# The last layer's first lower projections by Strassen's algorithm, with the plain pairs' rows written as right factors

## The chip, the cores and the metric

The kernel runs on one core of a Trainium2 chip. The metric is the device time of one execution in microseconds (us); lower is better. The core's engines have queues of their own, each worked off in order, and meet by semaphores: TensorE (PE) multiplies, VectorE (DVE) and ScalarE (ACT) do elementwise work, GpSimd (POOL) does elementwise work and issues the DMAs that accumulate, SyncE (SP) issues the other loads.

## What is computed

A trunk of two layers over 512 tokens of 1024 features, all in float32: a Conformer convolution layer, then a layer with sliding-window attention, each followed by a SwiGLU feed-forward part with 2816 hidden features. The change lies in the feed-forward part of the last layer:

```python
D_FF = -(-8 * D_MODEL // (3 * 256)) * 256        # 2816
...
def swiglu_ffn(x, w_up, w_down):
    gate, up = jnp.split(x @ w_up, 2, axis=-1)
    return (jax.nn.silu(gate) * up) @ w_down
...
        h = h + swiglu_ffn(rmsnorm(h, norm_ffn[l]), ffn_w_up[l], ffn_w_down[l])
    return rmsnorm(h, norm_final)
```

## The kernel before

Every matmul of float32 data is done as three matmuls on split values: a value is a high part (rounded for the PE) and a remainder, and the product is high x high, high x remainder and remainder x high (`mm3`, lines 383 to 385). Weights are split on the chip: `split_chunk` casts a chunk of 128 x 1024 to its high part `whi` on ACT and subtracts it on DVE to give `wlo` (line 307). There are five buffers of each, four (`raw`) for what is loaded, and a cast into a buffer waits until the PE has read the chunk that lay there before.

The 2816 hidden features are 11 pairs of 256. A pair's upper projection is done in one of two ways. *Plain* (`ffn_up`): four chunks, 24 matmuls of 512 columns each; `evac` scales the four banks on DVE (lines 637 and 639), applies SiLU on ACT (638), multiplies on POOL (640) and splits the result into `hid`. *By Strassen's algorithm* (`ffn_prod`): the 512 tokens are cut into two halves, and seven products of 24 matmuls of 256 columns take the place of eight; a product needs a combination of weight blocks and a combination of activations. I call them upper products 0 to 6. The blocks of a weight matrix lie in a tile `blocks` (three blocks, two buffers) and two `raw` tiles; SP loads them, and POOL issues DMAs that add one block onto another (`load_block`, line 241); two sums are left to DVE (lines 256 and 257). The activations' combinations, the right factors, are built once per layer by `right_factors`, called step by step through a background list while the plain pairs run; the two tiles it works in come from the pools `blocks` and `hid`.

The lower projection, too, is plain (`down_group`: chunks of 24 matmuls of 512 columns) or by Strassen's algorithm (`down_prod`: for each of two row groups, seven products of 18 matmuls of 256 columns over three pairs; I call those of the first group lower products, in the order 0, 1, 3, 2, 4, 5, 6). Its right factors are combinations of the hidden rows by token halves, kept by the class `Rights`: `finish` makes four subtractions of 256 columns on DVE and splits the seven factors of a pair.

Before, the last layer's part 0 (pairs 0 to 2) has two plain pairs, whose factors for the upper products are built meanwhile, then pair 2 by Strassen's algorithm, then a plain lower projection over the three pairs. Parts 1 and 2 (pairs 3 to 8) use Strassen's algorithm both ways, and pairs 9 and 10 end in a plain lower projection that is joined with the final normalization.

The order in each queue is not the order of the source: the scheduling layer moves instructions by its own estimate of their times, and the order is then fixed in the program.

Of the kernel before, what the change touches and what calls it, by code (L numbers as in the profile page):

```python
# [35 lines left out]
PLAIN = (2, 2)  # L36
# [21 lines left out]
def chunk_plan():  # L58
    plan = []

    def pw1():
        plan.extend(("pw1", ct, half) for ct in range(KT) for half in range(2))

    def pw2():
        for g in range(2):
            for kp in range(KT // 2):
                plan.append(("pw2", kp, g))

    def ups(layer, lo, hi):
        for pair in range(lo, hi):  # L70
            if pair >= PLAIN[layer]:
                plan.extend(("prod", layer, pair, j) for j in range(7))
                continue
            for half in range(2):
                for which in range(2):
                    plan.append(("up", layer, pair, half, which))

    def ffn(layer, lo, hi):
        ups(layer, lo, hi)
        if lo:  # L80
            plan.extend(("dprod", layer, (lo, ms), j) for ms in range(2) for j in D_ORDER)
            return
        for g in range(2):
            for kp in range(lo, hi):
                plan.append(("down", layer, kp, g))

    pw1()
    pw2()
    for part in HALVES0:
        ffn(0, *part)  # L90
    for part in range(2):
        for half in range(2):
            plan.append(("kv", part, half))
    for quarter in range(4):
        for half in range(2):
            plan.append(("q", half, quarter))
    for part in range(2):
        for g in range(2):
            for kp in range(2):
                plan.append(("o", part * 2 + kp, g))  # L100
    for part in HALVES1:
        ffn(1, *part)
    ups(1, *LAST)
    for kp in range(*LAST):
        for g in range(2):
            plan.append(("down", 1, kp, g))
    return plan
# [77 lines left out]
def hybrid_trunk(ctx: ExitStack, tc: tile.TileContext, xT, W, prm_in, wdw_in, rnd_in, sinks, relb, onehot, fin, out):  # L185
    nc = tc.nc
# [161 lines left out]
    def flush():  # L348
        for j in jobs:
            for _ in j[0]:  # L350
                pass
        jobs.clear()
        tick(1 << 30)
# [146 lines left out]
    def split(dst, src):  # L500
        nc.scalar.copy(dst[0], src)  # L501
        nc.vector.tensor_sub(dst[1], src, f32(dst[0]))  # L502
# [25 lines left out]
    def ffn_part(layer, part, xg, rms=None, on_h=None, right=None):  # L528
        lo, hi = (HALVES0, HALVES1)[layer][part]
        if lo:  # L530
            down_prod(layer, lo, ffn_prod(layer, lo, hi, xg, Rights()), on_h)
            return
        plain = PLAIN[layer]
        hids = [ffn_up(layer, lo, plain, xg, rms)]
        if hi > plain:
            flush()
            hids.append(ffn_prod(layer, plain, hi, right))
        hid = [t for pairs, n in zip(hids, (plain - lo, hi - plain)) for t in (pairs[i] for i in range(2 * n))]
        for g in range(2):
            banks = down_group([(("down", layer, kp, g), 2 * (kp - lo)) for kp in range(lo, hi)], lambda kt: hid[kt])  # L540
            for m in range(4):
                t = h[g * 4 + m]
                nc.vector.tensor_add(t, banks[m], t)
                if on_h is not None:
                    on_h(g * 4 + m)

    def halves(t):
        return t.rearrange("p (m s) -> p m s", m=2)
# [78 lines left out]
                for m in range(2):  # L627
                    on_h(4 + 2 * ms + m)

    def ffn_up(layer, lo, hi, xg, rms):  # L630
        hid = Act(2 * (hi - lo))

        def evac(pair, banks):
            rs_bc = rms.step2()
            for m in range(2):
                t1, t2 = temp(), temp()
                nc.vector.tensor_mul(t1, banks[m], rs_bc)
                nc.scalar.activation(t1, t1, AF.Silu)
                nc.vector.tensor_mul(t2, banks[2 + m], rs_bc)
                nc.gpsimd.tensor_mul(t2, t1, t2)  # L640
                split(hid[2 * (pair - lo) + m], t2)

        for pair in range(lo, hi):
            banks = [bank() for _ in range(4)]
            for half in range(2):
                for which in range(2):
                    whi, wlo = get("up", layer, pair, half, which)
                    order = [(k, m) for k in range(4) for m in range(2)]
                    if half == 1:
                        order = [(k, m) for m in range(2) for k in range(4)]  # L650
                    for k, m in order:
                        sl = slice(m * P, (m + 1) * P)
                        mm3(banks[which * 2 + m], (whi[:, k, sl], wlo[:, k, sl]), xg[half * 4 + k],
                            half == 0 and k == 0, half == 1 and k == 3)
                    if half == 0 and which == 1:
                        rms.step1()
            evac(pair, banks)
        return hid
# [122 lines left out]
    with conv_stage:  # L781
# [309 lines left out]
        b = None  # L1091
# [381 lines left out]
```

## Time and profile before

| | before |
|---|---|
| time, median of 3 runs | 1048.17 us (1048.11 to 1048.46) |
| the profiled execution: its time, its span | 1048.24 us, 1046.5 us |
| PE: chain that ended last, share | 86% |
| last layer's feed-forward part on PE, from the first plain pair to the last upper product | 695 to 1006 us |
| HBM traffic | 148 GB/s over the span |

The profile is one execution. Busy shares are per engine; a matmul's own duration is longer than the distance to the next one, since matmuls overlap. A release in square brackets names what ended an engine's idle time and how long that was.

### The profile page before, as it was taken

Reading aid. Unit: us, or ns where it says so; the run is one execution under the profiler, and the core shown is the slowest. Engines: PE = TensorE matmul, PEld = TensorE weight load, DVE = VectorE, ACT = ScalarE, POOL = GpSimd, SP = SyncE. Lnnn points to the kernel's source line nnn. Section 1 sums busy time; section 2 is a strip of 40 time slices with the busy share of each in tenths; the row PEclk is TensorE's granted clock in tenths of the full one; section 3 lists DMA queues with packets and bytes.
Section 4 is the critical chain, followed back from the end, with each engine's and each line's share of the span. In section 5 each row is a group of like instructions: output and inputs, shape, how many; then the busy total and the mean of one; then the engine's idle time right before and its main releaser. Section 6 shows DMA issues by size and latency. Waiting matters only on the chain.

```text
span 1046.5 us, 17698 instructions
## 1 busy us (share of the span) xinstructions
PE 1028.9 (98%) x7034; PEld 917.4 (88%) x7034; DVE 811.2 (78%) x1125; ACT 540.7 (52%) x835; POOL 237.8 (23%) x256
## 2 busy tenths in 40 slices
PE   9999999999999999999979999999999999999997
PEld 7756568888999999999969777788989999999996
DVE  8889867588789888978993767577965888788863
ACT  6565745353554455455562766354633554554443
POOL 0799801321010100101060433141100001010000
PEclk9999999999999999999999999999999999999999
DMA  7756533465557965976362211441654549667612
GB/s 254 201 146 164 133 114 92 129 161 141 167 159 173 281 165 124 260 194 161 82 217 72 72 41 42 147 135 41 188 174 122 141 121 263 174 153 176 178 46 81
DMA packets 51054, 153.95 MB, mean 147 GB/s; under 512 B 5979, under 2 KB 8844, under 8 KB 50956
## 3 DMA queue, kind: packets, MB, share of 16 engines
q1 hardware_dynamic: 41756, 124.79, 37.1%
q0 software_dynamic: 8064, 26.74, 15.1%
q10 hardware_dynamic: 1152, 1.29, 0.4%
q8 instruction: 55, 0.90, 0.3%
q14 instruction: 27, 0.22, 0.1%
HBM read 148.46 MB, written 6.83 MB: 148 GB/s over the span
## 4 chain that ended last, share of the span: by engine, by line
PE 86%; DVE 3%; issue 1%; POOL 1%; ACT 1%; POOLq 0%; ACTq 0%
PE bank L384 23%; PE bank L385 23%; PE bank L383 22%; PE bank L375 16%; PE bank L1402 2%; DVE quad L498 1%; DVE wlo L307 1%; DVE bank L318 1%; POOL quad L959 0%; DVE quad L991 0%; PE bank L472 0%; PE bank L489 0%; PE bank L1392 0%; DVE h L596 0%; POOL quad L978 0%
## 5 line engine op out<-in xcount | busy, mean ns | idle before, releaser
L384 PE MATMUL bank<-quad,whi 128*128 128x256 f32 (+1 forms) x1572 | 473.7, 303 | 4.1 <-DVE quad L498 4.1
L385 PE MATMUL bank<-quad,wlo 128*128 128x256 f32 (+1 forms) x1572 | 470.4, 303 | 0.0
L383 PE MATMUL bank<-quad,whi 128*128 128x256 f32 (+1 forms) x1572 | 465.9, 302 | 1.9 <-ACT quad L497 1.9
L384 PEld LDWEIGHTS bank<-quad,whi 128*128 128x128 f32 x1572 | 300.5, 191 | 16.2 <-DVE quad L498 4.9
L383 PEld LDWEIGHTS bank<-quad,whi 128*128 128x128 f32 x1572 | 298.6, 191 | 13.5 <-ACT quad L497 2.3
L385 PEld LDWEIGHTS bank<-quad,wlo 128*128 128x128 f32 x1572 | 298.8, 191 | 10.9
L307 ACT CAST whi<-raw 128x1024 fp32r<-128x1024 f32 (+1 forms) x184 | 183.9, 1002 | 230.7 <-PE bank L384 145.0
L307 DVE TENSOR_TENSOR wlo<-raw,whi 128x1024 fp32r<-128x1024 f32 (+1 forms) x184 | 223.0, 1218 | 95.2 <-ACT whi L307 92.7
L375 PE MATMUL bank<-quad,whi 128*128 128x512 f32 x512 | 160.7, 395 | 1.0 <-DVE quad L318 0.8
L241 POOL DMA_DIRECT2D blocks<-in_W_dram x56 | 49.0, 907 | 464.9 <-DMA blocks<-in_W_dram 197.9
L307 ACT CAST whi<-blocks 128x1024 fp32r<-128x1024 f32 (+1 forms) x84 | 81.7, 972 | 107.7 <-PE bank L384 79.5
L375 PEld LDWEIGHTS bank<-quad,whi 128*128 128x128 f32 x512 | 94.6, 188 | 26.8 <-issue 4.8
L307 DVE TENSOR_TENSOR wlo<-blocks,whi 128x1024 fp32r<-128x1024 f32 (+1 forms) x84 | 95.0, 1135 | 9.8 <-ACT whi L307 8.9
L375 PE MATMUL bank<-quad,wlo 128*128 128x512 f32 x256 | 99.9, 390 | 0.1
L959 POOL TENSOR_TENSOR quad<-quad 128x512 f32<-128x512 f32 x53 | 76.6, 1445 | 14.0 <-ACT quad L957 10.8
L375 PEld LDWEIGHTS bank<-quad,wlo 128*128 128x128 f32 x256 | 48.0, 188 | 10.9 <-DVE wlo L318 0.4
L462 POOL TENSOR_TENSOR tmp<-tmp,tmp 128x512 f32<-128x512 f32 x21 | 35.7, 1702 | 88.2 <-ACT tmp L460 86.3
L596 DVE TENSOR_TENSOR h<-h,bank 128x512 f32<-128x512 f32 x70 | 46.9, 682 | 10.6 <-PE bank L385 10.5
L1301 POOL TENSOR_SCALAR sc<-sc,sm 128x256 f32<-128x256 f32 (+1 forms) x64 | 31.7, 515 | 71.3 <-DVE sm L1299 71.2
L957 ACT ACTIVATE quad<-apad,wdw 128x512 f32<-128x512 f32 x53 | 36.9, 718 | 20.0 <-POOL quad L959 20.0
L502 DVE TENSOR_TENSOR quad<-tmp,quad 128x512 fp32r<-128x512 f32 (+1 forms) x62 | 41.5, 671 | 4.0 <-ACT quad L501 4.0
L501 ACT CAST quad<-tmp 128x512 fp32r<-128x512 f32 (+1 forms) x62 | 35.2, 585 | 13.8 <-POOL tmp L640 7.6
(189 smaller groups left out, 1226.2 us busy)
## 6 DMA issues: line engine op xcount, KB each, us to landing
raw<-in_W_dram SPq DMA_DIRECT2D x109, 512.0 KB, 3.8
blocks<-in_W_dram SPq DMA_DIRECT2D x54, 512.0 KB, 5.6
blocks<-in_W_dram POOLq DMA_DIRECT2D x36, 512.0 KB, 8.0
blocks<-in_W_dram SPq DMA_DIRECT2D x30, 384.0 KB, 3.9
raw<-in_W_dram SPq DMA_DIRECT2D x21, 384.0 KB, 3.8
blocks<-in_W_dram POOLq DMA_DIRECT2D x20, 384.0 KB, 5.9
shifted<-rowsd SPq DMA_DIRECT2D x16, 262.0 KB, 4.4
shifted<-rowsd SPq DMA_DIRECT2D x12, 260.0 KB, 5.4
```

What stands on the lines that cost most here:

```text
L241: nc.gpsimd.dma_start(f[:, j, 0:w], part(1 - j, 1 - j), accum_op=ALU.add)
L307: done = (nc.scalar.copy(hi, r).ins, lo_engine[0].tensor_sub(lo, r, f32(hi)).ins)
L375: turn[0] = nc.tensor.matmul(*args, **kw).ins
L383: nc.tensor.matmul(out, w[0], x[0], start=start, stop=False, **kw)
L384: nc.tensor.matmul(out, w[0], x[1], start=False, stop=False, **kw)
L385: nc.tensor.matmul(out, w[1], x[0], start=False, stop=stop, **kw)
L462: eng.tensor_add(sq, self.acc[eng], sq)
L501: nc.scalar.copy(dst[0], src)
L502: nc.vector.tensor_sub(dst[1], src, f32(dst[0]))
L596: nc.vector.tensor_tensor(t, t, src.rearrange("p (m s) -> p m s", m=2), op=op)
L957: nc.scalar.mul(pr, src, self.tap(j))
L959: nc.gpsimd.tensor_add(to, acc, pr)
```

## The change

In the last layer, part 0 now ends with the lower projection by Strassen's algorithm over pairs 0, 1 and 2, so that all three parts of that layer do. `ffn_part` gives the plain pairs a `Rights` object; `evac` then writes the product of gate and value by token halves into two tiles (`parts`) and calls `finish` on them, and `ffn_prod` adds pair 2 to the same object. The plan of weight chunks follows: 14 factors of three blocks of 128 x 256 take the place of six chunks. The first layer is unchanged (its part 0 has no pair beyond the plain ones).

```diff
--- before.py
+++ after.py
@@ -77,7 +77,7 @@
 
     def ffn(layer, lo, hi):
         ups(layer, lo, hi)
-        if lo:
+        if hi > PLAIN[layer]:
             plan.extend(("dprod", layer, (lo, ms), j) for ms in range(2) for j in D_ORDER)
             return
         for g in range(2):
@@ -531,11 +531,12 @@
             down_prod(layer, lo, ffn_prod(layer, lo, hi, xg, Rights()), on_h)
             return
         plain = PLAIN[layer]
-        hids = [ffn_up(layer, lo, plain, xg, rms)]
         if hi > plain:
+            hid = ffn_up(layer, lo, plain, xg, rms, Rights())
             flush()
-            hids.append(ffn_prod(layer, plain, hi, right))
-        hid = [t for pairs, n in zip(hids, (plain - lo, hi - plain)) for t in (pairs[i] for i in range(2 * n))]
+            down_prod(layer, lo, ffn_prod(layer, plain, hi, right, hid), on_h)
+            return
+        hid = ffn_up(layer, lo, hi, xg, rms)
         for g in range(2):
             banks = down_group([(("down", layer, kp, g), 2 * (kp - lo)) for kp in range(lo, hi)], lambda kt: hid[kt])
             for m in range(4):
@@ -627,18 +628,26 @@
                 for m in range(2):
                     on_h(4 + 2 * ms + m)
 
-    def ffn_up(layer, lo, hi, xg, rms):
-        hid = Act(2 * (hi - lo))
+    def ffn_up(layer, lo, hi, xg, rms, rights=None):
+        hid = Act(2 * (hi - lo)) if rights is None else rights
 
         def evac(pair, banks):
             rs_bc = rms.step2()
+            if rights is not None:
+                parts = [halves(temp()) for _ in HALF]
             for m in range(2):
                 t1, t2 = temp(), temp()
                 nc.vector.tensor_mul(t1, banks[m], rs_bc)
                 nc.scalar.activation(t1, t1, AF.Silu)
                 nc.vector.tensor_mul(t2, banks[2 + m], rs_bc)
-                nc.gpsimd.tensor_mul(t2, t1, t2)
-                split(hid[2 * (pair - lo) + m], t2)
+                if rights is None:
+                    nc.gpsimd.tensor_mul(t2, t1, t2)
+                    split(hid[2 * (pair - lo) + m], t2)
+                    continue
+                for b, tok in zip(parts, HALF):
+                    nc.gpsimd.tensor_mul(b[:, m], t1[:, tok], t2[:, tok])
+            if rights is not None:
+                rights.finish(*parts)
 
         for pair in range(lo, hi):
             banks = [bank() for _ in range(4)]
```

The places in the queues, with the changed program's names. On PE, at upper product 3 of pair 2 (`whi1024`, `wlo1025`, right factor `quad1001`); before, the high and low weights of that product were `whi1017`, `wlo1018`, and what follows is the first plain lower chunk (`whi1028`):

```order
L383 MATMUL bank1011_7361<-quad999_7304,whi1017_7397 128x256
L384 MATMUL bank1011_7361<-quad999_7304,whi1017_7397 128x256
L385 MATMUL bank1011_7361<-quad999_7304,wlo1018_7398 128x256
L383 MATMUL bank1033_7585<-quad955_7025,whi1028_7519 128x512
L384 MATMUL bank1033_7585<-quad956_7026,whi1028_7519 128x512
L383 MATMUL bank1034_7586<-quad955_7025,whi1028_7519 128x512
L384 MATMUL bank1034_7586<-quad956_7026,whi1028_7519 128x512
```

With the change the first lower product (`whi1033`, right factors of pair 0 in `quad982` and `quad983`, of pair 1 in `quad1009` and `quad1010`) follows there, and upper product 2 (`whi1022`) behind it:

```order
L383 MATMUL bank1016_7385<-quad1001_7315,whi1024_7429 128x256
L384 MATMUL bank1016_7385<-quad1001_7315,whi1024_7429 128x256
L385 MATMUL bank1016_7385<-quad1001_7315,wlo1025_7430 128x256
L383 MATMUL bank1042_7627<-quad982_7187,whi1033_7547 128x256
L384 MATMUL bank1042_7627<-quad983_7188,whi1033_7547 128x256
L385 MATMUL bank1042_7627<-quad982_7187,wlo1034_7548 128x256
L383 MATMUL bank1042_7627<-quad1009_7361,whi1033_7547 128x256
L384 MATMUL bank1042_7627<-quad1010_7362,whi1033_7547 128x256
L385 MATMUL bank1042_7627<-quad1009_7361,wlo1034_7548 128x256
```

Upper product 2 stood ahead of upper product 3 before, and eight matmuls of the plain lower chunk behind it; now twelve of the first lower product stand between upper products 3 and 2.

Further on, on PE, the last matmuls of upper product 2 and what follows, with the change: two matmuls of the second lower product (`whi1037`), then upper product 4 (`whi1026`):

```order
L384 MATMUL bank1014_7383<-quad998_7284,whi1022_7400 128x256
L385 MATMUL bank1014_7383<-quad998_7284,wlo1023_7401 128x256
L383 MATMUL bank1043_7628<-quad982_7187,whi1037_7583 128x256
L384 MATMUL bank1043_7628<-quad983_7188,whi1037_7583 128x256
L383 MATMUL bank1014_7383<-quad1002_7318,whi1026_7459 128x256
L384 MATMUL bank1014_7383<-quad1002_7318,whi1026_7459 128x256
```

Before, upper product 4 (`whi1020`) followed the eight matmuls of the lower chunk and nothing stood between it and upper product 5.

On ACT at the same time, before: casts of weights (line 307), copies of product banks (737, 742, 733), SiLU (638, 740) and the high parts of hidden rows (501):

```order
L501 CAST quad955_7025<-tmp1002_7335 128x512
L307 CAST whi1026_7490<-blocks973_7130 128x1024
L501 CAST quad955_7025<-tmp1004_7343 128x512
L307 CAST whi1028_7519<-raw996_7298 128x1024
L742 COPY tmp1013_7363<-bank1009_7359 128x512
L740 ACTIVATE tmp1012_7362<-tmp1012_7362 128x512
L307 CAST whi1031_7554<-raw1014_7364 128x1024
L733 COPY tmp1024_7486<-bank1011_7361 128x512
L307 CAST whi1038_7591<-raw1019_7427 128x1024
```

And with the change, where 677 are high parts of right factors of the upper products, and 746, 751 are the copies of product banks:

```order
L641 ACTIVATE tmp1007_7354<-tmp1007_7354 128x512
L307 CAST whi1033_7547<-raw1020_7389 128x768
L501 CAST quad1009_7361<-tmp1003_7345 128x512
L677 CAST quad1012_7376<-hid954_7024 128x1024
L677 CAST quad1013_7380<-hid954_7024 128x1024
L746 COPY tmp1017_7386<-bank1014_7383 128x512
L501 CAST quad1009_7361<-tmp1011_7363 128x512
L501 CAST quad1009_7361<-tmp1004_7346 128x512
L307 CAST whi1037_7583<-raw1021_7393 128x768
L749 ACTIVATE tmp1017_7386<-tmp1017_7386 128x512
L751 COPY tmp1018_7387<-bank1014_7383 128x512
```

In the place of `whi1028` come `whi1033` and `whi1037`, with the two last right factors, the copy behind upper product 0 and three high parts of pair 1's factors between them.

On POOL, before: the products of pairs 0 and 1 (640) and the accumulating DMAs of pair 3's blocks (241):

```order
L640 TENSOR_TENSOR tmp979_7174<-tmp978_7173,tmp979_7174 128x512
L640 TENSOR_TENSOR tmp981_7182<-tmp980_7181,tmp981_7182 128x512
L640 TENSOR_TENSOR tmp1002_7335<-tmp1001_7334,tmp1002_7335 128x512
L241 DMA blocks1040_7619<-in_W_dram 128x1024 x2
L640 TENSOR_TENSOR tmp1004_7343<-tmp1003_7342,tmp1004_7343 128x512
```

And with the change (648 are the products by token halves):

```order
L648 TENSOR_TENSOR tmp1003_7345<-tmp1005_7347,tmp1006_7348 128x256
L648 TENSOR_TENSOR tmp1004_7346<-tmp1005_7347,tmp1006_7348 128x256
L241 DMA blocks1019_7388<-in_W_dram 128x768 x2
L648 TENSOR_TENSOR tmp1003_7345<-tmp1007_7354,tmp1008_7355 128x256
L648 TENSOR_TENSOR tmp1004_7346<-tmp1007_7354,tmp1008_7355 128x256
L241 DMA blocks1035_7578<-in_W_dram 128x768 x2
```

The DMAs that stand there are now those of the two row groups of the lower projection (`blocks1019`, `blocks1035`); DVE's sum of blocks (256) behind upper product 6's weights waits for the first of them.

## The prediction

> **What bounds the kernel now.** I read the page first, then who waits for whom, then busy time by stretch, then single queues around the place of the change. All times in us count from the span's start.
>
> ```profile
> span 1046.5 us, 17698 instructions
> PE 1028.9 (98%) x7034; PEld 917.4 (88%) x7034; DVE 811.2 (78%) x1125; ACT 540.7 (52%) x835; POOL 237.8 (23%) x256
> PE bank L384 <- DVE quad L498: 4.1, 2, 3.8
> PE bank L383 <- ACT quad L497: 1.9, 1, 1.9
> ```
>
> TensorE (PE) is the bound: 98% busy, and its longest waits in the whole program are 3.8 and 1.9 us. So a matmul less is time gained, and a wait added is time lost, one for one. The profiled execution took 1048.24 us, 0.07 above the median of 1048.17; I add to 1048.24.
>
> ```profile
> core 0: us, PE busy (x) PEld busy (x) DVE busy (x) ACT busy (x) POOL busy (x), PEclk, DMA share, GB/s
> 717.00:740.00 23.00, 23.00 (x103) 19.05 (x102) 23.00 (x25) 13.27 (x16) 3.54 (x2) 1.00 0.11 36
> 740.00:763.00 23.00, 23.00 (x181) 22.42 (x180) 20.50 (x21) 12.10 (x17) 6.97 (x6) 1.00 0.86 263
> 763.00:796.00 33.00, 33.00 (x159) 27.80 (x158) 17.90 (x20) 8.21 (x9) 0.00 (x0) 1.00 0.37 104
> 856.00:871.00 15.00, 15.00 (x128) 15.00 (x128) 15.00 (x23) 7.61 (x11) 1.71 (x2) 1.00 0.53 169
> ```
>
> The changed stage is here: up to 740.6 PE runs the two plain pairs, then the seven upper products of pair 2, and from about 760 the plain lower projections. PE never waits. But VectorE (DVE) has no free time from 717 to 740 and 2.5 us from 740 to 763; the plain lower projections (763 to 796) are where it recovers, with 17.90 of 33 us busy. The change puts its new work ahead of the recovery and thins the recovery itself.
>
> **The change part by part.** First what it saves.
>
> ```profile
> 719.73 0.39 PE L384 MATMUL bank<-quad,whi 128*128 128x512 f32 x1
> ...
> 734.91 0.39 PE L385 MATMUL bank<-quad,wlo 128*128 128x512 f32 x1
> 815.74 0.28 PE L383 MATMUL bank<-quad,whi 128*128 128x256 f32 x1
> ...
> 818.74 0.28 PE L384 MATMUL bank<-quad,whi 128*128 128x256 f32 x1
> ```
>
> These are the first and last of 68 matmuls of 512 columns and of 26 of 256. Start to start that is 15.18/67 = 0.2266 us and 3.00/25 = 0.1200 us. The plain lower projections are 6 chunks of 24 matmuls: 144 x 0.2266 = 32.6 us. Strassen's are 14 factors of 18: 252 x 0.1200 = 30.2 us. **Saved: 2.4 us.** The Trainium skill (TensorE: Matmul & The Clock Gate, Back-to-back issue gap) gives a gap of columns over 2.4 GHz plus 2.5 ns, so 215.8 and 109.2 ns, by which the saving would be 3.6 us; the trace has 11 ns more on either size, and I go by the trace.
>
> Then what it adds. The rows of the plain pairs become seven right factors each: per pair four subtractions of 256 columns and splits of 3 x 512 + 256 columns where there were two splits of 512. Multiplications on GpSimd (POOL) become four of 256 per pair instead of two of 512. Weights come as 14 splits of 768 instead of 6 of 1024, with 4 sums of blocks on DVE, and 14 additions to h replace 8. I cost that last group at nothing once the stage runs: the stretch 856 to 871 has the same lower products at DVE 15.00 of 15 us and PE does not wait. If that cover is a little short, a few tenths come on top.
>
> At the entry to the stage there is no such cover, and there the order of the queues decides. PE now has, right behind upper product 3 of pair 2 (weights whi1024), twelve matmuls of the first lower product (whi1033), then upper product 2, then two matmuls of the second lower product (whi1037), then upper product 4. The built program says what each waits for: whi1033 is cast into the buffer that whi1024 leaves, whi1037 into that of whi1022, upper product 2. So each cast can only start when the PE is already at the instruction that needs it.
>
> ```profile
> 743.33 0.28 PE L385 MATMUL bank<-quad,wlo 128*128 128x256 f32 x1
> 743.59 1.05 ACT L307 CAST whi<-raw 128x1024 fp32r<-128x1024 f32 x1 [1.94 <-PE bank L384]
> L307 ACT CAST whi<-raw 128x768 fp32r<-128x768 f32 x40 | 33.4, 835 | 39.5 <-PE bank L384 33.3 <-ACT whi L307 4.4 <-ACT tmp L742 1.8
> L307 DVE TENSOR_TENSOR wlo<-raw,whi 128x768 fp32r<-128x768 f32 x40 | 38.1, 953 | 6.5 <-ACT whi L307 6.3
> ```
>
> Upper product 0 ends with the matmul of 743.33; the cast into its buffer starts 0.26 later, 0.14 after the next matmul was due. A cast of 768 takes 0.83 and its remainder on DVE 0.95. **The least that the first place can cost** is 0.14 + 0.83 + 0.1 = 1.1, and 0.8 more for the remainder: 1.9 us. The least at the second is 1.1, and 1.3 behind it, since upper product 4 needs the bank of product 2 copied, and that copy stands behind the cast and an activation (0.63 + 0.58) in ScalarE's (ACT's) queue. Together 4.3 us against 2.4 saved.
>
> Mostly it will cost more, because DVE waits in the middle of this for a sum of blocks, whose blocks come by two DMAs in sequence (SP, then an accumulating one from POOL), and their buffer is the one that the upper factors are built in.
>
> ```profile
> 739.12 2.34 DVE L669 TENSOR_TENSOR quad<-blocks,quad 128x1024 fp32r<-128x1024 f32 x2
> 743.73 2.02 DVE L307 TENSOR_TENSOR wlo<-blocks,whi 128x1024 fp32r<-128x1024 f32 x1
> 741.49 0.80 SPq L240 DMA_DIRECT2D blocks<-in_W_dram  x2
> 745.43 0.92 POOL L241 DMA_DIRECT2D blocks<-in_W_dram  x1 [0.76 <-DMA blocks<-in_W_dram]
> blocks<-in_W_dram SPq DMA_DIRECT2D x30, 384.0 KB, 3.9
> blocks<-in_W_dram POOLq DMA_DIRECT2D x20, 384.0 KB, 5.9
> ```
>
> Now the buffer comes free at 739.12 + 2.34 = 741.46 and SP issues at once. With the change these stand ahead of the same point on DVE: four operations of 256 columns, one more split of 512, one multiplication of 512 by the scale, one weight remainder of 1024.
>
> ```profile
> L574 DVE TENSOR_TENSOR tmp<-tmp,tmp 128x256 f32<-128x256 f32 x15 | 6.3, 419 | 0.0
> L502 DVE TENSOR_TENSOR quad<-tmp,quad 128x512 fp32r<-128x512 f32 x52 | 37.3, 719 | 4.0 <-ACT quad L501 4.0
> L669 DVE TENSOR_TENSOR quad<-blocks,quad 128x1024 fp32r<-128x1024 f32 x6 | 7.1, 1210 | 0.0
> L501 ACT CAST quad<-tmp 128x512 fp32r<-128x512 f32 x52 | 31.1, 619 | 13.7 <-POOL tmp L640 7.6 <-DVE tmp L717 3.5 <-DVE tmp L1256 2.6
> L749 ACT ACTIVATE tmp<-tmp 128x512 f32<-128x512 f32 x18 | 11.3, 628 | 0.1
> L742 ACT COPY tmp<-bank 128x512 f32<-128x512 f32 x18 | 10.5, 582 | 0.0
> 743.37 1.30 POOL L640 TENSOR_TENSOR tmp<-tmp,tmp 128x512 f32<-128x512 f32 x1 [18.41 <-DVE tmp L639]
> ```
>
> In a full queue DVE operations overlap by 0.07, so 4 x 0.35 + 2 x 0.61 + 1.14 = 3.8 us, and 0.8 for two POOL products that now fall there (the 2.02 us of 743.73, beside the POOL product of 743.37, against 1.21): the buffer is free at 746.0. Load 3.9: 749.9. POOL issues at 750.2; landing 5.9: 756.1. DVE's sum of blocks 0.88, a factor's remainder 1.14, a factor's subtraction 0.42: 758.5. ACT's cast of that factor 0.62, then the cast whi1037 0.83, with 0.1 at each hand-over: the second lower product starts at 760.2. Without waits PE would be there 108 matmuls after 740.58, at 753.5. **Delay there 6.7 us**, in which the first place's wait is contained. (That place lags too: its fourth matmul and the next need a factor of pair 1 whose POOL product now stands behind the two DMA issues of 750.2, so it ends near 755.6 instead of 750.6.) Then DVE's next factor remainder and an addition (1.14 + 0.61, to 760.3), the activation 0.63 and the copy 0.58: upper product 4 starts at 761.6 instead of 760.4, **1.2 us** more. At the end of pair 2, 17 of the 36 matmuls that cover its last right factors have been pulled forward; the chain behind product 6 (0.61 + 0.35 + 0.88 + 0.35 + 0.68 and 0.2 of hand-overs, 3.1 us) outlasts the 22 matmuls left before the remainder is needed (2.6 us), and a bank waits for an addition to h: **0.8 us**, between 0 and 1.2. Waits 6.7 + 1.2 + 0.8 = 8.7, less 2.4: plus 6.3 us.
>
> What these unknowns are worth: the accumulating DMA takes 7.8 to 12 us (median 9.4) where the queues are full:
>
> ```profile
> DMA to landing us min/median/max: 7.8/9.4/12.0
> ```
>
> These are 512 KB loads between 745 and 773; 9.4 instead of 5.9 adds 3.5. If the loads come early, the 4.3 us above remain. I take 5.9, the row of the same size.
>
> **The clock.** The trace of before shows once what such waits do to PE's clock.
>
> ```profile
> 541.37 0.73 PE L383 MATMUL bank<-quad,whi 128*128 128x512 f32 x2 [1.92 <-ACT quad L497]
> 545.88 0.80 PE L384 MATMUL bank<-quad,whi 128*128 128x512 f32 x1 [3.78 <-DVE quad L498]
> 544.00:554.30 10.30, 8.42 (x29) 7.46 (x30) 4.99 (x6) 1.12 (x2) 3.91 (x3) 0.51 0.55 224
> ```
>
> Two waits with two matmuls between, then 10.3 us at a granted clock of 0.51. By the sum above PE has, from 749.2 to 754.6, four matmuls, and from 749.2 to 761.6 only 38 (4.6 us of 12.4). If the clock halves near 753 and stays so for 10.3 us, upper product 2 (24 matmuls, 2.9 us) takes 2.9 longer; the rest of the slow time falls mostly into waits that are there anyway. Price plus 3, between 0 and 5. The Trainium skill (TensorE: Matmul & The Clock Gate, What's actually happening) has the clock fall to half after one idle window of about 3.4 us, and 10.3 us is three such windows, so that far the trace agrees.
>
> **The rivals.**
> - *Forecast: waits and half clock.* 1048.24 + 6.3 + 3.0 = 1057.5, from 1055 to 1061.5. For it: the queues' order and the stretch at 544. Chance 0.45.
> - *Waits alone.* The scattered matmuls keep the clock up: 1054.5, from 1052 to 1057. Against it: two matmuls between two waits did not keep it at 544. Chance 0.30. The Trainium skill (TensorE: Matmul & The Clock Gate, What's actually happening), taken at its word of a whole idle window, would give this case, since no 3.4 us here is wholly empty; the trace's stretch at 544 was not wholly empty either.
> - *Only the two buffers wait*, the blocks landing before DVE comes to them: 4.3 + 0.8 - 2.4 = plus 2.7, 1050.9; against it, load and accumulation alone are 9.8 us from a buffer that DVE holds to 746. Chance 0.09.
> - *Faster.* PE finds its weights cast: the mechanism is ACT at the two casts, which would have to follow the release within the time of a matmul. It decides from the point at which the waits there sum to under 2.4 us. Then 1045.8. The trace has 1.1 for the shortest such hand-over, and there are two, one with a remainder behind it. Chance 0.07.
> - *Heavier*, accumulations at 9.4 us and the half clock lasting over the next pair: 6.3 + 3.5 + 5, about 1063. Chance 0.09.
>
> **How the numbers follow.** Predicted is the first case, 1057.5. The range 1051.0 to 1061.5 takes the first two, and leaves out faster, no change and the heavier one, nearly 2 in 10. About 0.2%, 2.1 us, is what a measurement of this kernel can tell from no change: faster (under 1046.1) 0.06, same 0.07 (the faster case with a small wait, or the third with a shorter one), slower 0.87.
>
> **What would show it.** Right: the list of PE's waits, empty in this stretch before, names ACT's casts of 768, ACT's copies of product banks and DVE's right factors, some 8 us in all, between 749 and 775; the DVE queue has a gap of 3 us or more ended by a DMA at the first sum of blocks of 768; the matmuls' count falls by 144 of 512 and rises by 252 of 256; a second stretch with a clock near 0.5 begins near 753. Wrong: PE without waits there, or a clock of 1.00 throughout (then 1054.5); a wait in the next pairs, where I expect none.

## The result, and the profile after

| | before | with the change |
|---|---|---|
| median of the timed runs | 1048.33 us (6 runs, 1048.11 to 1049.70) | 1055.52 us (6 runs, 1053.85 to 1056.73) |
| ratio, 95% interval | | 1.0064 (1.0051 to 1.0077) |
| the profiled execution: its time, its span | 1048.24 us, 1046.5 us | 1053.85 us, 1052.1 us |

The change makes the kernel slower by 7.2 us. The forecast was 9.3 us more than the profiled execution of before, 1057.5, with a range from 1051.0 to 1061.5.

The head of the page and the list of PE's waits of the changed kernel (line waited at, who ended it: sum, count, longest):

```profile
span 1052.1 us, 17990 instructions
PE 1028.4 (98%) x7142; PEld 921.4 (88%) x7142; DVE 829.8 (79%) x1161; ACT 548.7 (52%) x849; POOL 247.7 (24%) x264
```

```profile
PE bank L384 <- DVE quad L498: 4.1, 2, 3.8
PE bank L383 <- ACT whi L307: 3.2, 2, 2.4
PE bank L385 <- DVE wlo L307: 2.5, 1, 2.5
PE bank L383 <- ACT quad L497: 1.9, 1, 1.9
...
PE bank L383 <- ACT tmp L751: 0.5, 1, 0.5
PE bank L384 <- DVE hid L502: 0.4, 1, 0.4
```

PE has 108 matmuls more, 252 - 144, as forecast. The lines of 4.1 and 1.9 us are the old waits at 541 to 546. New are the four others, 3.2 + 2.5 + 0.5 + 0.4 = 6.6 us, all in pair 2. Where they stand shows PE's timeline (start, duration, row, in brackets the idle time ahead and what ended it):

```profile
749.64 0.39 PE L383 MATMUL bank<-quad,whi 128*128 128x256 f32 x1 [2.40 <-ACT whi L307]
752.63 0.58 PE L385 MATMUL bank<-quad,wlo 128*128 128x256 f32 x1 [2.48 <-DVE wlo L307]
760.11 0.39 PE L383 MATMUL bank<-quad,whi 128*128 128x256 f32 x1 [0.80 <-ACT whi L307]
761.11 0.39 PE L383 MATMUL bank<-quad,whi 128*128 128x256 f32 x1 [0.50 <-ACT tmp L751]
```

The first two are the first lower product (cast, then remainder), the third is the second lower product, the fourth is upper product 4, which waits for a copy of product 2's bank: the forecast's places, one by one. The clock by stretch (PE's busy time behind the length, the granted clock third from the end):

```profile
747.40:750.90 3.50, 0.50 (x2) 0.30 (x2) 3.44 (x4) 2.28 (x4) 3.21 (x5) 1.00 0.93 274
750.90:757.70 6.80, 5.07 (x23) 4.97 (x24) 6.80 (x10) 3.31 (x5) 0.88 (x2) 0.50 0.99 257
757.80:775.00 17.20, 15.48 (x125) 14.87 (x124) 12.46 (x21) 8.32 (x14) 0.78 (x1) 1.00 0.39 78
```

From 750.9 the clock is halved for 6.8 us. PE works in 5.1 of them, so about half of that, 2.5 us, is lost to the clock. 6.6 of waits, 2.5 of clock and small gaps of some 1.5 us, less the 2.4 saved, make 8.2: by the trace the way from the first matmul of upper product 0 to the last of 256 columns became 8.0 us longer. The profiled execution as a whole is 5.6 us longer, since the older half-clock stretch near 543 happened to be one of 6.8 us in place of 10.2. So this stage begins 2.1 us earlier than before (738.45 in place of 740.58), which has to be borne in mind when a time here is held against one of the forecast.

So sum and places fit. What the forecast gave as their cause does not: the chain through DVE's wait for a sum of blocks. DVE's timeline of the changed kernel:

```profile
747.46 0.69 DVE L640 TENSOR_TENSOR tmp<-bank,rsbc 128x512 f32<-128x512 f32 x1 [1.33 <-POOL tmp L648]
...
749.00 2.71 DVE L307 TENSOR_TENSOR wlo<-blocks,whi 128x1024 fp32r<-128x1024 f32 x1
751.63 0.94 DVE L307 TENSOR_TENSOR wlo<-raw,whi 128x768 fp32r<-128x768 f32 x1
...
753.44 0.94 DVE L256 TENSOR_TENSOR raw<-blocks,raw 128x768 f32<-128x768 f32 x1
```

The sum of blocks (256) runs at 753.44 with no idle time ahead: the accumulating DMA for it, issued at 747.36, landed 5.7 us later, some 0.4 us before the sum. So that chain was about as long as DVE's own queue, and it was not what DVE stood still for. Instead DVE stands still at 747.46, at a multiplication that reads a bank and the scale. POOL writes neither of these, so what DVE waits for is the buffer that it writes, one of five temporary ones, still being read by POOL's products. Those, and ACT behind DVE:

```profile
741.43 5.99 POOL L648 TENSOR_TENSOR tmp<-tmp,tmp 128x256 f32<-128x256 f32 x2 [14.35 <-DVE tmp L642]
747.36 1.82 POOL L241 DMA_DIRECT2D blocks<-in_W_dram  x2
748.96 1.66 POOL L648 TENSOR_TENSOR tmp<-tmp,tmp 128x256 f32<-128x256 f32 x2
```

```profile
748.24 0.63 ACT L641 ACTIVATE tmp<-tmp 128x512 f32<-128x512 f32 x1 [2.91 <-DVE tmp L640]
748.78 0.81 ACT L307 CAST whi<-raw 128x768 fp32r<-128x768 f32 x1
```

Two products of 256 columns took POOL 5.99 us here. The first of them alone took 5.30, beside a DVE without a gap from 741.18 to 746.13, and ended 0.6 us after DVE had come to its standstill; the second took 0.73. The next two took 1.66, and there it was DVE's remainder beside them that took 2.71. ACT stands 2.91 us before the SiLU with the cast of the first lower product's weights queued behind it; upper product 3, which leaves the weights' buffer, had issued its last matmul at 747.0 (71 x 0.120 after 738.45), so the cast, possible 0.26 later, came 1.5 late. Its remainder stood behind one of 2.71 us in place of 1.21, beside POOL's 1.66: 1.5 late. That is how the forecast's least of 1.9 us at this place became 4.9. The Trainium skill (SBUF — State Buffer, SBUF: two separate sides) has GpSimd and a DVE operation with two inputs in SBUF exclude one another for a whole instruction; 5.30 and 2.71 agree with it, though the 5.30 span several DVE operations of at most 1.21 us, not one.

Two readings of this trace were open. *Queue order (Q)*: the lower products stand where their buffers have only just been left, and cost what they wait there. *A late producer*: DVE, ACT and POOL are behind at that point, and PE waits once, whatever stands there; within it *DVE's backlog (D)*, *POOL's products (P)* or *the temporary buffers (T)*: with the change a plain pair takes up to seven (two gates, two values, two halves, one for the differences), and pair 2's copies come from the same five. These three can act together: a buffer that DVE waits for comes free late because POOL's product, which reads it, is long.

### The profile page after: what moved, and what is told of

It reads as the page before. It is cut to its first block, busy times and chain, and to the rows that moved or that the text cites. A ratio compares the mean times of both kernels' runs of the same rounds, so it can differ in the third digit from the quotient of the medians.

```text
span 1052.1 us, 17990 instructions
## 1 busy us (share of the span) xinstructions
PE 1028.4 (98%) x7142; PEld 921.4 (88%) x7142; DVE 829.8 (79%) x1161; ACT 548.7 (52%) x849; POOL 247.7 (24%) x264
## 4 chain that ended last, share of the span: by engine, by line
PE 82%; DVE 6%; POOL 2%; issue 1%; ACT 1%; POOLq 0%; DVEq 0%; ACTq 0%
PE bank L384 21%; PE bank L383 21%; PE bank L385 21%; PE bank L375 16%; PE bank L1411 2%; DVE wlo L307 2%; POOL tmp L648 1%; DVE quad L498 1%; DVE bank L318 1%; POOL quad L968 0%; DVE h L597 0%; DVE quad L1000 0%; PE bank L489 0%; DVE hid L1175 0%; PE bank L472 0%
## 5 line engine op out<-in xcount | busy, mean ns | idle before, releaser
L241 POOL DMA_DIRECT2D blocks<-in_W_dram x60 | 52.5, 912 | 467.5 <-DMA blocks<-in_W_dram 147.3
L307 ACT CAST whi<-blocks 128x1024 fp32r<-128x1024 f32 (+1 forms) x90 | 86.6, 962 | 109.0 <-PE bank L384 82.9
L307 DVE TENSOR_TENSOR wlo<-blocks,whi 128x1024 fp32r<-128x1024 f32 (+1 forms) x90 | 101.2, 1129 | 5.3 <-ACT whi L307 4.2
L597 DVE TENSOR_TENSOR h<-h,bank 128x512 f32<-128x512 f32 x84 | 56.1, 679 | 13.1 <-PE bank L385 13.0
L384 PE MATMUL bank<-hid,whi 128*128 128x256 f32 x168 | 47.5, 285 | 0.4 <-DVE hid L502 0.4
L385 PE MATMUL bank<-hid,wlo 128*128 128x256 f32 x168 | 46.9, 281 | 0.0
```

Of the source, the lines that this page charges most:

```text
L241: nc.gpsimd.dma_start(f[:, j, 0:w], part(1 - j, 1 - j), accum_op=ALU.add)
L307: done = (nc.scalar.copy(hi, r).ins, lo_engine[0].tensor_sub(lo, r, f32(hi)).ins)
L384: nc.tensor.matmul(out, w[0], x[1], start=False, stop=False, **kw)
L385: nc.tensor.matmul(out, w[1], x[0], start=False, stop=stop, **kw)
L597: nc.vector.tensor_tensor(t, t, src.rearrange("p (m s) -> p m s", m=2), op=op)
```

## The experiments

Each was timed against the kernel before on the same chip, but not all on one chip, so that runs are compared by their ratios. "Waits" is the sum of PE's list between 690 and 820 us; "half clock" is the granted clock's record after 700 us, without the end of the program.

| run | median us | ratio to before (95%) | waits us | half clock us |
|---|---|---|---|---|
| the change | 1055.52 | 1.0064 (1.0051 to 1.0077) | 6.6 | 6.8 |
| e1 all lower products behind 6 | 1056.69 | 1.0092 (1.0076 to 1.0108) | 8.2 | 10.2 |
| e2a the first behind 2 | 1055.35 | 1.0079 (1.0065 to 1.0094) | 6.8 | 6.8 |
| e2b second and third behind 6 | 1054.60 | 1.0065 (1.0049 to 1.0081) | 6.9 | 6.8 |
| e3 busy wait | 1055.32 | 1.0073 (1.0057 to 1.0089) | 2.5, and 4.8 filled | 3.4 |
| e4 one pair bare | 1050.88 | 1.0028 (1.0017 to 1.0039) | 3.8 | 3.4 |
| e5 two pairs bare | 1051.17 | 1.0034 (1.0022 to 1.0046) | 3.7 | 3.4 |
| e6 products on DVE | 1056.13 | 1.0078 (1.0066 to 1.0090) | 8.4 | 10.2 |
| e7 products of 512 | 1051.59 | 1.0032 (1.0020 to 1.0044) | 4.7 | 6.8 |
| e8 halves in place | 1053.00 | 1.0040 (1.0025 to 1.0055) | 4.8 | 6.8 |
| e9 in place, one piece | 1049.63 | 1.0019 (1.0008 to 1.0031) | 3.0 | 0 |
| e10 in place, free order | 1048.48 | 1.0009 (0.9999 to 1.0019) | 2.0 | 0 |
| e11 buffers back | 1054.16 | 1.0060 (1.0046 to 1.0074) | 6.3 | 6.8 |

### Moving the products: e1, e2a, e2b

The end of each upper product is kept in `ends`, and the first matmul of each step of a held lower product may not be placed ahead of it:

```diff
     def mm3(out, w, x, start, stop, **kw):
-        nc.tensor.matmul(out, w[0], x[0], start=start, stop=False, **kw)
+        with tc.issue_after(hold[0]) if hold[0] is not None else nullcontext(): nc.tensor.matmul(out, w[0], x[0], start=start, stop=False, **kw)
...
+        last_mm[0] = nc.tensor.matmul(out, w[1], x[0], start=False, stop=stop, **kw).ins
...
-                    product(j, w, dst, ks, ks[0] == 0, j == 1 and ks[-1] == last)
+                    hold[0] = ends[6] if (layer, lo, ms) == (1, 0, 0) else None; product(j, w, dst, ks, ks[0] == 0, j == 1 and ks[-1] == last); hold[0] = None
...
+                ends[j] = last_mm[0]
```

This is e1; e2a holds only the first (`ends[2] if j == 0`), e2b only the others (`ends[6] if j`).

> Holds the three lower products of the first row group that had been pulled into pair 2 behind upper product 6 (first, second and third lower product), so that PE runs the seven upper products in one piece; nothing else is changed. Theory Q (the order of PE's queue makes the waits: a lower product stands where its weight buffer has only just been left): no PE wait over 0.5 us between 740 and 775, no half clock there, and the time is the one before less the 2.4 us of matmuls saved, plus 0 to 1.2 for the last right factors: 1045.9 to 1047.2. Rival D (DVE is overloaded by the right factors of the plain pairs, and PE has to wait for it wherever the products stand): waits of 4 us or more reappear in upper products 2 to 6 or behind them, 1052 to 1056.

> Moves only the first lower product, from behind upper product 3 to behind upper product 2 (24 matmuls, 2.9 us later); the second place stays as in the changed kernel. Theory Q: the 4.9 us of the first place (2.40 + 2.48) shrink by the 2.9 us of cover to about 2.0, and with only one short wait there the clock stays up (another 2.2 us gained): 1050 to 1052.5. Rival D: waits of the same sum elsewhere, 1054 to 1056.

> Moves only the second and third lower product behind upper product 6; the first lower product stays behind upper product 3 as in the changed kernel. Theory Q: the waits at the second place (0.80 + 0.50) go, the 4.9 us and the half clock of the first stay: 1053.5 to 1054.5. Rival D: the same time as the changed kernel, 1055 to 1056. If the first place alone carries the loss, this run stays within 1.5 us of the changed kernel while the one that moves the first product gains 3 us or more.

Q falls as the account of the whole loss. With the upper products in one piece the time did not fall to 1046 or 1047; it is 1056.69. With the first lower product moved (e2a) it is 1055.35, where Q had 1050 to 1052.5. The time of e2b alone, 1054.60, lies between the two theories and decides nothing. The waits list of e1 in that stage:

```profile
PE bank L383 <- ACT tmp L746: 5.8, 1, 5.8
PE bank L383 <- ACT tmp L751: 2.4, 1, 2.4
```

The wait now stands at upper product 2, which adds into the bank of product 0 and needs that bank copied first (746). ACT's timeline of e1 says why the copy is late:

```profile
751.31 0.63 ACT L641 ACTIVATE tmp<-tmp 128x512 f32<-128x512 f32 x1 [2.91 <-DVE tmp L640]
751.85 0.82 ACT L307 CAST whi<-raw 128x768 fp32r<-128x768 f32 x1
753.05 0.62 ACT L501 CAST quad<-tmp 128x512 fp32r<-128x512 f32 x1 [0.39 <-POOL tmp L648]
753.58 1.99 ACT L677 CAST quad<-hid 128x1024 fp32r<-128x1024 f32 x2
755.47 0.57 ACT L746 COPY tmp<-bank 128x512 f32<-128x512 f32 x1
```

Product 0 had ended at 744.4, but the copy stands in ACT's queue behind the same SiLU with the same 2.91 us of idle time. In all four orders (the change, e1, e2a, e2b) PE waits 6.6 to 8.2 us in sum; only the place changes. So the pulled-forward product of the change stands in front of a wait of about the same size, which is there without it too.

### Filling the wait: e3

40 matmuls of 256 columns, whose results are overwritten, stand ahead of the first lower product:

```diff
+                    if (layer, lo, ms, j, ks[0]) == (1, 0, 0, 0, 0):
+                        q, prev = hid.factor(0, 0)[0], ends[3]
+                        for _ in range(40):
+                            with tc.issue_after(prev):
+                                prev = nc.tensor.matmul(dst[:, 0:256], q[:, 0:P], q, start=True, stop=True,
+                                                        skip_group_check=True).ins
                     product(j, w, dst, ks, ks[0] == 0, j == 1 and ks[-1] == last)
```

> Adds 40 matmuls of 256 columns, on tiles that are ready, ahead of the first lower product in PE's queue (their bank is overwritten by its first matmul); they fill the 4.9 us that PE waits there. Theory C (the idle time at the first place halves the clock, and that costs 2 to 3 us on upper product 2): 40 x 0.120 = 4.8 us of matmuls in place of 4.9 us of waits, no half clock near 751, and 1052.5 to 1053.5. Rival (the clock was not what cost; the remaining loss is in the waits alone): 1055 to 1056.

The clock stayed up through the first place, and yet the time is that of the change. PE came to the second lower product earlier and waited there longer, 1.69 us in place of 0.80, and the clock was halved for 3.4 us behind it:

```profile
760.53 0.39 PE L383 MATMUL bank<-quad,whi 128*128 128x256 f32 x1 [1.69 <-ACT whi L307]
```

As a price of the clock this is inconclusive, since the half clock was not removed but moved. It speaks for the late producer: what PE gains, it waits for next.

### How much DVE work: e4, e5

On e1's order. `bare` is 1 or 2; the matmuls read the high part in place of the remainder, so that these two kernels leave out a part of the result:

```diff
+            nc.scalar.copy(dst[0], src)
+            if not (self.bare and len(self.hi) <= self.bare):
+                nc.vector.tensor_sub(dst[1], src, f32(dst[0]))
...
-            return tuple(t[k][:, self.SLOT[j], :] for t in (self.hi, self.lo))
+            return tuple(t[k][:, self.SLOT[j], :] for t in (self.hi, self.hi if k < self.bare else self.lo))
```

> On the order with all seven upper products in one piece (its waits: 5.8 and 2.4 us, 1056.7). Leaves out the remainders of pair 0's right factors: three subtractions of 512 columns and one of 256 on DVE, 3 x 0.61 + 0.35 = 2.2 us; the matmuls that would read them read the high parts instead, so PE's work is unchanged. Theory D (DVE's queue is full ahead of the stage, and PE waits once for its backlog, wherever the products stand): the first wait falls from 5.8 to about 3.6, time 1053.9 to 1055.0. Rival A (the waits come from the order in ACT's queue and the products on GpSimd (POOL), not from the amount of DVE work): waits and time within 0.8 us of 1056.7.

> The same, and pair 1's remainders left out too: 4.4 us less on DVE in all. Pair 1's remainders stand behind the first place and ahead of the second. Theory D: the first wait about 3.6 as with one pair, the second wait (2.4) gone: 1051.5 to 1053.5. Rival A: within 0.8 us of 1056.7.

The 2.2 us of pair 0 (e4) bring more than either theory expected: 0.0064 of the time against e1, some 6.7 us, in place of about 2.2. Waits of 8.2 became 3.8, and 10.2 us of half clock 3.4. So what was left out ahead of the stage counts, and more than one for one. The same amount in pair 1 brings nothing (1.0034 against 1.0028). A pure backlog of DVE would have shrunk by it as well at the second wait. And whoever leaves a remainder out also frees the buffer that it reads, so that these two runs cannot part D from T.

### The products: e6, e7, e8

On e1's order. In e6 the products go to DVE; in e7 POOL makes one of 512 columns in place (`tensor_mul(t2, t1, t2)`, as before the change), and the factors are cut from it; e8 is e7 with two of 256 in place. In both `finish_rows` takes one buffer for the differences, so that a pair holds five in place of seven. The edits of e6 and of e7:

```diff
-                    nc.gpsimd.tensor_mul(b[:, m], t1[:, tok], t2[:, tok])
+                    nc.vector.tensor_mul(b[:, m], t1[:, tok], t2[:, tok])
```

```diff
-                for b, tok in zip(parts, HALF):
-                    nc.gpsimd.tensor_mul(b[:, m], t1[:, tok], t2[:, tok])
-            if rights is not None:
-                rights.finish(*parts)
+                nc.gpsimd.tensor_mul(t2, t1, t2)
+                parts.append(t2)
+            if rights is not None:
+                rights.finish_rows(*parts)
```

> On the same order: the products of gate and value of pairs 0 and 1 on DVE in place of POOL (8 of 256 columns, 8 x 0.35 = 2.8 us more on DVE, 15 us less on POOL). Theory P (POOL's products, held up beside a busy DVE to 5.99 us for two, make the chain of pair 1 late, and DVE's 1.3 us wait and its remainder of 2.7 us beside them with it): 1052 to 1055. Theory D: DVE has 2.1 us more ahead of the first place and 1.3 less of waiting there: 1056.7 to 1058.5.

> On the same order: POOL makes one product of 512 columns per row block as before the change, and the right factors are cut from its result; two splits of 512 per pair become four of 256 (about 0.2 us more on DVE each, 0.4 to 0.5 per pair), and two temporary buffers fewer are held. Theory P: POOL's pairs of products shrink from 4.5, 2.5, 6.0, 1.7 us to near the 1.8 of before each, and the first wait by 1.3 to 3: 1053.5 to 1055.5. Theory D: 1056.5 to 1058.

> As the run with one product of 512 columns, but POOL again makes two products of 256 per row block, now in place, so that the two extra temporary buffers stay saved (three held per pair in place of the changed kernel's larger set). Theory T (the five temporary buffers are what binds: the products' tiles, the factors' tile and pair 2's copies together want more than five, and an engine whose buffer isn't free stands still with its queue behind it): as with 512, 1051 to 1052.6. Theory P (the length of POOL's products beside a busy DVE): back to 1054.5 to 1057.

Without POOL's products (e6) nothing is gained, although DVE's remainder beside them is back at 1.22 us. With one product of 512 and two buffers fewer (e7) the time is 0.0060 shorter than e1's, more than either theory expected, although DVE has more to do. With POOL's halves in place (e8) its products take 2.42 and 3.26 us for pair 1 where e7's take 1.30 and 2.13, but PE waits 4.8 us against 4.7, and the intervals of the ratios overlap. So between e7 and e8, which differ in the form of the products alone, P carries little: 0.0008 of the time, some 0.8 us, no more than the noise. And e8, with POOL's products of 256 as in the change and two buffers fewer, is still 0.0052 faster than e1. In e6 the forecast's chain does appear, on DVE's timeline:

```profile
757.02 0.96 DVE L256 TENSOR_TENSOR raw<-blocks,raw 128x768 f32<-128x768 f32 x1 [4.24 <-DMA blocks<-in_W_dram]
```

There DVE waits 4.24 us for the accumulating DMA. The chain exists; in the change its block had landed shortly before DVE came to it. That is also why e6 is no clean test of P: against e1, PE's first wait fell from 5.8 to 4.2 us, and the second, behind this gap of DVE, grew from 2.4 to 4.2.

### The buffers alone: e9, e10, e11

e9 and e10 make the factors in place, with as many operations of the same sizes on DVE as the change (four subtractions of 256, splits of 3 x 512 + 256), one product of 512 on POOL, and no buffer beside the rows'. e9 has e1's hold, e10 none. The slots of a factor are noted per pair:

```diff
+        def finish_rows(self, r0, r1):
+            self.slots.append((0, 1, 6, 3, 4, 2, 5))
+            self.add()
+            self.put(0, r0[:, 0:1])
+            self.put(1, r1)
+            nc.vector.tensor_sub(r0[:, 0], r0[:, 0], r0[:, 1])
+            nc.vector.tensor_sub(r0[:, 1], r1[:, 1], r0[:, 1])
+            self.put(3, r0)
+            nc.vector.scalar_tensor_tensor(r1[:, 1], r0[:, 0], -1.0, r1[:, 1], op0=ALU.mult, op1=ALU.subtract)
+            nc.vector.scalar_tensor_tensor(r1[:, 0], r1[:, 1], -1.0, r1[:, 0], op0=ALU.mult, op1=ALU.subtract)
+            self.put(5, r1)
```

e11 is e9 with fresh buffers again, three more per pair:

```diff
-            nc.vector.tensor_sub(r0[:, 0], r0[:, 0], r0[:, 1])
-            nc.vector.tensor_sub(r0[:, 1], r1[:, 1], r0[:, 1])
-            self.put(3, r0)
+            t = halves(temp())
+            nc.vector.tensor_sub(t[:, 0], r0[:, 0], r0[:, 1])
+            nc.vector.tensor_sub(t[:, 1], r1[:, 1], r0[:, 1])
+            self.put(3, t)
...
-                nc.gpsimd.tensor_mul(t2, t1, t2)
+                p = t2 if rights is None else temp()
+                nc.gpsimd.tensor_mul(p, t1, t2)
```

> All seven upper products in one piece, one POOL product of 512 columns per row block, and the right factors of pairs 0 and 1 made in place: four subtractions of 256 and splits of 3 x 512 + 256 columns as in the change, but no buffer beside the two that hold the rows. Theory T: the waits of 4.7 us with 512 products fall to under 2.5: 1047.5 to 1050. Theory P: POOL's work is that of the run with 512, DVE's 0.9 us less: 1050.3 to 1051.8.

> The same factors in place, on the change itself with nothing held back, so that lower products are again pulled into pair 2 (two matmuls behind upper product 3, two behind 4, fifteen more behind 5). If the temporary buffers and DVE's backlog were the cause, it stands within 1 us of the run in one piece, 1047.5 to 1050; if the pulled-forward products cost by themselves through their weight buffers (forecast's minimum of 1.1 us each), 1.5 us or more above it.

> As the run with all seven upper products in one piece and the factors made in place, but the same operations write to fresh temporary buffers again: the product of gate and value to one buffer more per row block, the differences to one more, three more per pair, as many as the change holds. Every engine has the same number of operations of the same sizes as with the in-place factors; only what they wait for differs. Theory T (the five temporary buffers bind): most of the gain is lost again, 1053.5 to 1056.7, with PE waits of 5 to 8 us behind upper product 3. Theory D (the amount of DVE work alone, and the form of POOL's products): as with the in-place factors, 1049 to 1051.

The buffers count. e9 and e11 have the same operations of the same sizes on every engine, and differ by 0.0041 of the time, 4.3 us; only which buffers they write differs. PE's waits in that stage, first of e9, then of e11:

```profile
PE bank L384 <- DVE hid L502: 2.1, 2, 1.2
PE bank L383 <- ACT tmp L760: 0.9, 1, 0.9
```

```profile
PE bank L383 <- ACT tmp L757: 5.0, 1, 5.0
PE bank L383 <- ACT tmp L762: 1.3, 1, 1.3
```

The copy of upper product 0's bank on ACT, in e9 and in e11 (the stage begins at 740.0 and 740.9):

```profile
744.81 0.57 ACT L755 COPY tmp<-bank 128x512 f32<-128x512 f32 x1
```

```profile
754.05 0.58 ACT L757 COPY tmp<-bank 128x512 f32<-128x512 f32 x1
```

With the buffers saved it runs 4.8 us into the stage, with them taken again 13.1. The rest of e9's waits is what was expected of a short cover, the last right factors of pair 2 (DVE, 502), and DVE is still full, as the stretch of e9 from 740 to 775 shows (DVE is the third busy time, 34.97 of 35 us; the clock is 1.00):

```profile
740.00:775.00 35.00, 32.03 (x256) 30.84 (x255) 34.97 (x50) 19.97 (x29) 6.97 (x6) 1.00 0.64 161
```

e10 is the change with its loss gone: 1048.48, and no difference from before that can be measured. It saves the buffers and has POOL's product of 512, both at once. Two matmuls of a lower product still stand behind upper product 3 there (twelve in the change), and two behind 4, and the list of waits has 0.4 us for a cast. No kernel of the study beats the one before.

Three things are not settled. The first is how the buffers act. DVE's plain wait for a buffer is 1.33 us in the change, and in e11's stage there is none at all. What the trace of e11 does show is another order in the queues: the copy stands behind the factors' casts there and ahead of them in e9. That the scheduling layer makes this order by when it takes a buffer to be free is a reading that no run tested. The second is POOL: its four products of 512 took 12.4 us in e11 and 7.0 in e9, so that the buffers and the length of POOL's products were not parted there. The third is the rest. From e1 to e9 the ratio falls by 0.0073, some 7.7 us; 4.3 of that lie between e11 and e9, and the other 3.4 lie between e1 and e11, which hold seven buffers per pair each and differ in the form of POOL's products and in the order of the operations and of the buffers they take. A run with more than five buffers and nothing else changed was not made.

## Why the prediction held, and where it was wrong

- **What bounds** held: PE 98% busy, no slack, DVE without a gap from 717 to 740 ahead of the stage. A wait added was time lost.
- **Saved, 2.4 us**, held: +108 matmuls, and in the trace of e10 the stage (first matmul of upper product 0 to the last of 256 columns) is 0.6 us longer than before with 3.3 us in distances over the usual one, so PE's own work is 2.7 shorter, within 0.3 of the term.
- **The first place, at least 1.9 us**, was 4.9. The 3.0 above the least are 1.5 for a cast behind a late SiLU and 1.5 for a remainder beside POOL's product.
- **The delay of 6.7 us through the blocks** is the step that failed: "DVE waits in the middle of this for a sum of blocks". The sum ran at 753.44 without waiting; the gap of 3 us or more that was to show the forecast right is not there. The length of the chain was about right: from the start of the stage to the landing of the first accumulation 15.5 us were forecast (756.1 - 740.58), and it was 14.6 (some 753.1 - 738.45). What was missing is that DVE's own queue, held up by 1.33 us for a buffer and by 1.5 beside POOL's product, came to the sum no earlier. The second lower product stood at 760.11; without waits PE would have been there 108 matmuls after 738.45, at 751.4. So it was 8.7 us late, where the forecast had 6.7 and the clock on top; that 760.2 was forecast is a coincidence of the two starting points. The 8.7 are 4.9 at the first place, 2.5 of half clock, 0.8 of its own and half a us of small gaps. In the place of the failed step the runs put the temporary buffers (e9 against e11, 4.3 us), by a way that stays open. The prediction followed the weights' and the blocks' buffers and never counted these.
- **"each cast can only start when the PE is already at the instruction that needs it"** is true of the order, but did not set what PE lost: e1 and e2a took the first place away, and the waits stayed in sum. The forecast priced a position in PE's queue where the price hung on the engines behind it.
- **Upper product 4, 1.2 us, and the tail, 0.8**, measured 0.5 and 0.4; both mechanisms are in the list (751's copy, DVE 502).
- **The clock, plus 3**: the mechanism was right, 12.4 us behind the start of the stage as forecast (753 after 740.58, 750.9 after 738.45); 6.8 us of it in place of 10.3 and 2.5 us lost. That it came without a window wholly idle was right too. The Trainium skill (TensorE: Matmul & The Clock Gate, What's actually happening) names one idle window of about 3.4 us; here PE had two waits of 2.40 and 2.48 us with matmuls between, so by this trace the window need not be wholly idle.
- **Of the rivals**, "waits alone" has 1055.52 in its range too; it falls with the clock, not with the time. "Only the two buffers wait" had the condition that came true, the blocks landing before DVE came to them, and had been given 0.09; what it had wrong is the price, since the first place cost 4.9 in place of 1.9 and the clock fell. "Faster" falls with the waits' sum of 6.6 against its limit of 2.4. That the next pairs do not wait was right.

So the forecast was right in sign and near in size, 9.3 against 7.2 us. The sign and the places follow from its order of PE's queue. That the size came near is luck in its largest term: a producer that it had not counted was late by about as much as the one that it had.

## What to carry to other kernels

Before a wait is priced at its place in the consumer's queue, count the live buffers of every pool that the new code draws on, small temporary ones too: rewriting a step in place was worth 4.3 us here with not one operation less. To tell a bad place from a late producer, move the consumer: if the waits' sum stays (6.6 to 8.2 us in four orders), the cause is behind it. A wait filled or shortened alone can uncover the next one, as in e3 and e6.

## What the runs showed of the hardware that was not expected

- POOL's product of 256 columns took between 0.73 and 5.30 us: 5.30 beside a DVE without a gap, 0.73 while DVE stood still. A DVE remainder of 1024 columns took 2.71 beside two products that took 1.66 together, and 1.21 alone. For pair 1 a product of 512 took 1.30 and 2.13 us in e9, 3.61 and 1.93 in e11.
- The half clock came in stretches of 3.4 or 6.8 us in this stage, and after a single wait of 1.69 us (e3) or 2.5 (e4) too, while 1.6 us (e10), and 1.2 and 0.9 (e9), left the clock at 1.00.
